# Output projection of the mixer: where its split weights are made, and in which order ACT, DVE and SP issue around it

## The chip, the cores and the metric

The kernel runs on one core of a Trainium2 chip. The metric is the time of one execution on the device in microseconds. The engines are TensorE (PE; its weight loads are a row of their own, PEld), VectorE (DVE), ScalarE (ACT), GpSimd (POOL) and SyncE (SP). SP and POOL issue most of the DMA transfers. Each engine works through its own queue in order, and an instruction that waits holds everything behind it on that engine.

## The reference, cut to what matters

One layer over 512 positions and 1024 channels, all in float32. The part around the change is the projection of the merged branches into the residual, the norm before the MLP, and the MLP's up projection:

```python
merged = gate_a * y_a + gate_b * y_b
x = x + jnp.einsum('bsd,de->bse', merged, w_out[i])

h2 = rmsnorm(x, norm_ffn_g[i])
up = jnp.einsum('bsd,df->bsf', h2, w_up[i])
up = causal_depthwise_conv(up, conv_w[i], conv_b[i])
act = jax.nn.gelu(up[..., :D_FF]) * up[..., D_FF:]
x = x + jnp.einsum('bsf,fd->bsd', act, w_down[i])
```

## The kernel before, in words

**Split operands.** Each float32 product is made of three TensorE products of shorter numbers: an operand is split into a high part (`hi`, a rounded copy made by ACT) and a low part (`lo`, the operand less `hi`), and the product is lo x hi + hi x lo + hi x hi. The low part of a weight is made in one of two ways. Either DVE subtracts (`tensor_tensor` with `ALU.subtract`), or, where the code says `"dma"`, ACT writes `-hi` into the low tile and POOL issues a DMA that adds the raw weight to it (`G.dma_start(lo, raw, accum_op=ALU.add)`). `load_w` (L145) does this for a weight that SP has just loaded; its cast is L153, its negation L156, its accumulating DMA L157, its subtraction L159. `m_split` (L1110) does the same for weights that lie in SBUF: cast L1115, negation L1117, DMA L1118, subtraction L1120. `pieces_T` (L192) loads and splits two pieces of 128 x 1024 for one pair of column blocks of the up projection; its arguments `sub` and `sub2` say how the first and the second piece's low parts are made, and the second goes as the first where `sub2` is left out.

**The projection by seven products.** The 512 x 1024 by 1024 x 1024 projection is a 2 x 2 block product done with seven products in place of eight. `w_out`'s four quarters `b11`, `b12`, `b21`, `b22` lie in two large tiles; `m_combine` forms their sums and differences in place on DVE, and `m_split` splits each. Written order of the weights: w1 and w6 (made during the stage before), w2, w5, w7, w4, w3. `m_product` (L1186) issues one product: two row halves (`rs`), each of four steps (`q`) of three matmuls of 128x512; after a half's last step it calls an evacuation. The activations' operands lie in tiles called slot and quad, the weights in whi/wlo (five pairs) and xhi/xlo (one pair), and the three sets of accumulators are the banks x, y and z. Products that end a row half of the result go through `m_rows` (L1218): DVE adds the bank to the residual x1 (`evac_x1`, L1171), ACT sums the squares (`square_sum`, L457), and `rms_rows` (L460) makes the norm: DVE adds two half sums (L463), a root is made with one ACT instruction between small DVE ones (L386, L391 to L394), and DVE scales the row block by it into `hn` (L468, twice). What `rms_rows` returns, `rest[rb]`, is called later: it transposes `hn` on TensorE (L421), ACT copies the high parts (L380) and DVE makes the low parts (L381) of `h2T`, the up projection's activation.

**What fills the norms' time.** Between those row blocks TensorE gets other work: a product with `w_ple` (`pp`, in steps, evacuated by ACT and stored by POOL), then the first pair's up products. `w_up0` holds the first pair's weights, gate and linear, two pieces each; `early` (L1263) runs them for rows 256 to 511 as soon as row blocks 2 and 3 are normed, and for rows 0 to 255 later.

**The up loop** (its jobs from `up_jobs`, L1320, and `down_jobs`, L1355; the loop at L1445) runs over jobs: for each pair of column blocks a gate job and a linear job, with four jobs of the down projection laid between those of every two pairs. A job's weights are loaded and split one job ahead. Up pieces go through three raw buffers; the down projection's four quarters of 512 KB (L1362) go to one tile and are combined by DVE (L1394, L1395 and so on) and split (`split_w`, L262).

**What sets the order.** The kernel is written in the Tile layer, whose scheduler chooses the order of each engine's instructions when the program is built, except where a `manual_schedule` region names an engine: then that engine issues the region's instructions in the order of the text. Where instructions from outside the region fall among them stays the scheduler's. Before the change one region, from the branch products (L1149) to `manual.close()` (L1274), names PE alone, and the up loop's names PE alone. ACT, DVE, POOL and SP are the scheduler's in both.

Of the kernel before, what the change touches and what calls it, by code (L numbers as in the profile page):

```python
# [15 lines left out]
P = 128  # L16
S = 512
D = 1024
NB = S // P
# [3 lines left out]
DFF = 2816  # L23
# [20 lines left out]
def hybrid_block(  # L44
# [7 lines left out]
    V, A, G, T = nc.vector, nc.scalar, nc.gpsimd, nc.tensor  # L52
# [3 lines left out]
    def kview(w):  # L56
        return w.rearrange("(k p) c -> p k c", p=P)

    w_in_v, w_a_v, w_b_v = kview(w_in[0]), kview(w_a[0]), kview(w_b[0])
    w_out_v, w_up_v, w_down_v = kview(w_out[0]), kview(w_up[0]), kview(w_down[0])  # L60
# [12 lines left out]
    def uid(s):  # L73
        state["n"] += 1
        return f"{s}_{state['n']}"
# [11 lines left out]
    def bank(tag=None):  # L87
        pool, bufs = state["psum"]
        if tag is None:
            tag = state["turn"][state["bank"] % len(state["turn"])]  # L90
            state["bank"] += 1
        return pool.tile([P, 512], F32, tag=tag, name=uid("bank"), bufs=bufs[tag])
# [11 lines left out]
    def tiny(tag, n=1, bufs=4):  # L104
        pool = state["late"] if tag in LATE else small
        return pool.tile([P, n], F32, tag=tag, name=uid(tag), bufs=bufs)
# [38 lines left out]
    def load_w(src, a, b, sub=None, later=None):  # L145


        raw = raw_tile(a, b)
        hi, lo = split_tiles(a, b)
        nc.sync.dma_start(raw, src)  # L150

        def split():
            A.copy(hi, raw)  # L153
            if sub == "dma":

                A.activation(lo, hi.bitcast(F32), AF.Copy, scale=-1.0)  # L156
                G.dma_start(lo, raw, accum_op=ALU.add)  # L157
                return
            (sub or V).tensor_tensor(lo, raw, hi.bitcast(F32), ALU.subtract)  # L159
        if later is not None:  # L160
            later.append(split)
        else:
            split()
        return hi, lo
# [27 lines left out]
    def pieces_T(wv, c0, sub=None, sub2=None):  # L192

        a = load_w(wv[:, 0:4, c0:c0 + 256], 4, 256, sub)
        b = load_w(wv[:, 4:8, c0:c0 + 256], 4, 256, sub2 or sub)
        return [[(*a, 0, 4, c), (*b, 4, 4, c)] for c in (0, P)]
# [186 lines left out]
    def rstd_of(ms, eps_scale):  # L383

        a = tiny("ra")
        V.tensor_scalar(a, ms, -0.5 * eps_scale, -0.5 * EPS, ALU.mult, ALU.add)  # L386
        return newton(a, ms, eps_scale, epst)
# [26 lines left out]
    def transpose_split(src, dst, rb, n=NK, keep=None):  # L414

        done = []
        for k0 in range(0, n, 4):
            w = min(4, n - k0)
            bk = bank()
            for k in range(w):  # L420
                T.transpose(bk[:, k * P:(k + 1) * P], src[:, (k0 + k) * P:(k0 + k + 1) * P], ident)  # L421
            at = (slice(None), slice(k0, k0 + w), slice(rb * P, rb * P + P))
            bk = bk[:, :w * P].rearrange("p (k r) -> p k r", k=w)
            split_out(dst, bk, at)
            done.append((at, bk))
        def copy():
            for at, bk in done:
                A.copy(keep[at], bk)
        return copy
# [24 lines left out]
    def square_sum(bk, src, tag):  # L454

        ss = tiny(tag, bufs=4)
        A.activation(bk, src, AF.Square, accum_out=ss)  # L457
        return ss

    def rms_rows(x_rb, ss, ss1, g_bc, scr, dst, rb, hn=None):  # L460


        V.tensor_tensor(ss, ss, ss1, ALU.add)  # L463
        y = rstd_of(ss, 1.0 / D)
        if hn is None:
            hn = scr.tile([P, D], F32, tag="hn", name=uid("hn"), bufs=2)
        for h in (0, 512):
            V.scalar_tensor_tensor(hn[:, h:h + 512], x_rb[:, h:h + 512], y,  # L468
                                   g_bc[:, h:h + 512], ALU.mult, ALU.mult)
        return lambda: transpose_split(hn, dst, rb)  # L470
# [12 lines left out]
    def quarter(tag, dt=F32R):  # L483

        return ph.tile([P, D], dt, tag=tag, name=uid(tag))
# [13 lines left out]
    ET = mybir.EngineType  # L499
# [112 lines left out]
    with tc.manual_schedule(engines={ET.PE}):  # L612
        proj_N(w_in_v[:, :, 4096:5120], 0, NK, hT, 1, evac_v, rb_outer=False, subs=subs_v1,
               after=forget)
    bk = bk_f[0]
# [29 lines left out]
    sums = [tuple(quarter(f"S{i}{t}").rearrange("p (k r) -> p k r", k=4) for t in "hl")  # L645
            for i in range(1, 5)]
# [67 lines left out]
    with tc.manual_schedule(engines={ET.PE}):  # L714
# [34 lines left out]
        bk = bank("sc")  # L749
# [7 lines left out]
        for g0 in (0, 4):  # L757
            steps(units, 6)
            bk = bank("sc")
# [227 lines left out]
    scr_es, scr = open_pool("scrC", "right")  # L987
# [67 lines left out]
    bk = bank()  # L1055
# [7 lines left out]
    A11, A12, A22, S1, S2, S3, S4 = range(7)  # L1063
# [41 lines left out]
    b11, b12, b21, b22 = b1[:, 0], b1[:, 1], b2[:, 0], b2[:, 1]  # L1105
# [4 lines left out]
    def m_split(b, subs=(None, None), first=None):  # L1110
        res = []
        for j in range(2):
            hi, lo = first if first and j == 0 else split_tiles(2, 512)
            raw = b[:, 2 * j:2 * j + 2]
            A.copy(hi, raw)  # L1115
            if subs[j] == "dma":
                A.activation(lo, hi.bitcast(F32), AF.Copy, scale=-1.0)  # L1117
                G.dma_start(lo, raw, accum_op=ALU.add)  # L1118
            else:
                V.tensor_tensor(lo, raw, hi.bitcast(F32), ALU.subtract)  # L1120
            res.append((hi, lo))
        return res
# [25 lines left out]
    manual = ExitStack()  # L1148
# [6 lines left out]
    scr_es, scr = open_pool("scrD", "right")  # L1155
    x1 = slot(6, F32).rearrange("p (b c) -> p b c", b=NB)
# [9 lines left out]
    gffn = scr.tile([P, D], F32, tag="gbc", name="gffn", bufs=1)  # L1166
# [5 lines left out]

    half = [None] * NB
    rest = [None] * NB

    def evac_x1a(bk, rb, ch):
        evac_x1(bk, rb, ch)
# [8 lines left out]
    def m_product(a, ws, acc, fresh, last, evac=None, qs=range(4), rs=range(2)):  # L1186

        if acc not in m_banks:
            m_banks[acc] = [bank({"x": "mm", "y": "sc", "z": "pt"}[acc]) for _ in range(2)]
        for r in rs:  # L1190
            bk = m_banks[acc][r]
            for q in qs:
                ah, al = (m_at(t, a, q)[:, P * r:P * r + P] for t in range(2))
                wh, wl = (w[:, q % 2, :] for w in ws[q // 2])
                for n, (l, m) in enumerate(((al, wh), (ah, wl), (ah, wh))):
                    T.matmul(bk, l, m, start=(fresh and q == 0 and n == 0),
                             stop=(q == 3 and n == 2), skip_group_check=not fresh)
            if evac:
                evac(bk, r)
# [18 lines left out]
    def m_rows(rows, ch):  # L1218

        def f(bk, r):  # L1220
            rb = rows + r
            evac_x1(bk, rb, ch)
            ss = square_sum(bk, x1[:, rb, 512 * ch:512 * ch + 512], f"s{ch}")
            rest[rb] = rms_rows(x1[:, rb, :], ss, half[rb], gffn, scr, h2T, rb)
        return f

    state["turn"], state["bank"] = ["pt", "pt", "pt", "av"], 0
    w1, w6 = MERGED
# [4 lines left out]
    m_combine(b11, b22, b11, ALU.subtract)  # L1233
    m_product(A12, w2, "x", False, True, qs=range(3))
    m_product(S2, w6, "y", True, False, m_add(2, 0), qs=[3])
    w5 = m_split(b11, (None, "dma"))
    m_product(A12, w2, "x", False, True, m_x, qs=[3])

    A.activation(epst2, half[1], AF.Sqrt)
    w7 = m_split(b12, ("dma", "dma"))  # L1240
    transpose_p(prow, pT, 0)
    m_product(S1, w5, "y", False, False, m_add(2, 1))
    w4 = m_split(b21)
    transpose_p(prow, pT, 2)
    m_product(S3, w7, "z", True, False, m_x2)
    h2T = tuple(k_view(slot(i)) for i in (0, 1))
    w3 = m_split(b22, ("dma", "dma"))
    pp = proj_N_steps(w_ple_v, 0, 2, pT, 1, evac_ple, subs=load_N(w_ple_v, 0, 2, 1))
    m_product(A22, w4, "z", False, True, m_rows(2, 0))
    w_up0 = [pieces_T(w_up_v, 0, V, "dma")]  # L1250
    state["turn"], state["bank"] = ["mm", "mm", "av", "pt", "pt", "pt"], 0
    steps(pp, 16)
    rest[2]()
# [1 line left out]
    state["turn"], state["bank"] = ["pt", "av", "pt", "pt"], 0  # L1255
    m_product(S4, w3, "y", False, True, m_rows(0, 1), rs=[0])
    rest[3]()
    m_product(S4, w3, "y", False, True, m_rows(0, 1), rs=[1])

    w_up0.append(pieces_T(w_up_v, DFF, V, "dma"))  # L1260
    up0 = [[bank(t) for _ in range(2)] for t in ("mm", "sc")]

    def early(n, i, rows=slice(256, S)):  # L1263
        run(proj_T_steps(w_up0[n][i], h2T, up0[n][i], rows))
# [6 lines left out]
    early(1, 1)  # L1271
    for i in range(2):
        early(0, i, slice(0, 256))
    manual.close()  # L1274
    state["turn"] = BANK_TURN
    scr_es.close()
# [5 lines left out]
    scr_es, scr = open_pool("scrE", "right")  # L1282
# [152 lines left out]
    jobs = up_jobs(0, done) + up_jobs(1, done)  # L1435
    jobs[0] = (lambda: w_up0[0], jobs[0][1])
    jobs[1] = (lambda: w_up0[1], jobs[1][1])
    for g in range(N_SEVEN):
        ups = up_jobs(2 * g + 2, done) + up_jobs(2 * g + 3, done)
        for pair in zip(ups, down_jobs(g)):  # L1440
            jobs += pair
    for q in range(2 * N_SEVEN + 2, NF // 2):
        jobs += up_jobs(q, done)

    with tc.manual_schedule(engines={ET.PE}):  # L1445
        ws = jobs[0][0]()
        for n, (_, products) in enumerate(jobs):
            nxt = jobs[n + 1][0]() if n + 1 < len(jobs) else None
            products(ws)
            ws = nxt  # L1450
# [88 lines left out]
    with tc.manual_schedule(engines={ET.PE, ET.Activation, ET.DVE}):  # L1539
        steps(proj_N_steps(w_pg_v, 0, NK, h3T, 1, evac_gate, subs=subs), 72)  # L1540

        rb = NB - 1
        r = ds(rb * P, P)
        for c0 in (0, 256):
            bk = bank()[:, 0:256]
# [53 lines left out]
```

## Time and profile before

| | us |
|---|---|
| median of three timed runs | 946.52 |
| lowest, highest | 944.88, 946.91 |
| the profiled execution | 943.61 |
| its span, first to last instruction | 941.8 |

The profile is of one execution. Its times count from the first instruction of that execution. The span is what the views below divide; what lies around it (1.8 us) is start and end of the execution. In the projection's stage, as the windows of the trace show it, TensorE is busy for 26.04 of the 30 us from 475 to 505 and for 19.95 of the 25 us from 530 to 555. In a timeline's row stand the start, the duration, the engine, the line, the operation, output <- inputs, and how many equal neighbours were merged; in brackets is the engine's idle time before it and what ended that. A line can be that of a helper, and then the tile's name says whose call it is.

### The profile page before, as it was taken

To read this page: it belongs to the slowest core of one execution; us is meant where nothing else is said; L and a number is where in the kernel's file an instruction comes from. 1 tells how busy PE (TensorE), PEld (TensorE's weight loads), DVE (VectorE), ACT (ScalarE), POOL (GpSimd) and SP (SyncE) were. 2 spreads that over 40 slices of the span, in tenths; PEclk is the share of its full clock that TensorE was granted. 3 is DMA by queue.
4 is the path that set the end of the run, shared out by engine and by line. 5 is a ranking of instruction groups with operands and counts; after the bars stand their busy time and mean duration, and the time that the engine had idled before them with its cause. 6 is when DMAs were issued, how large, how long until landed. Compare 5 with 4: busy or idle time off the path is not lost.

```text
span 941.8 us, 12133 instructions
## 1 busy us (share of the span) xinstructions
PE 920.9 (98%) x4375; PEld 767.3 (81%) x4375; DVE 630.2 (67%) x1152; ACT 562.2 (60%) x896; POOL 107.0 (11%) x158
## 2 busy tenths in 40 slices
PE   8999999999999999999998799999999999999996
PEld 7888888888888888888876798888888888888885
DVE  6886999577777767535674447667766767464654
ACT  7745675477677777536566466555555655545633
POOL 1000001400000010001121111010101110100124
PEclk9999999999999999999999989999999999999998
DMA  9533273755444456699777947675866865875422
GB/s 339 187 90 125 66 212 110 237 155 152 120 124 121 115 144 165 218 341 302 165 207 153 300 106 151 179 180 134 200 157 141 216 148 122 218 241 145 108 72 89
DMA packets 110088, 158.98 MB, mean 169 GB/s; under 512 B 6213, under 2 KB 71933, under 8 KB 110029
## 3 DMA queue, kind: packets, MB, share of 16 engines
q1 hardware_dynamic: 96380, 110.73, 36.1%
q0 software_dynamic: 13504, 46.96, 25.2%
q8 instruction: 34, 0.56, 0.2%
q10 hardware_dynamic: 144, 0.52, 0.1%
q14 instruction: 26, 0.20, 0.1%
HBM read 105.74 MB, written 12.62 MB: 126 GB/s over the span
## 4 chain that ended last, share of the span: by engine, by line
PE 90%; DMA 5%; issue 3%; DVE 1%; SPq 0%; ACT 0%; POOL 0%; DVEq 0%; POOLq 0%
PE bank L181 17%; PE bank L183 17%; PE bank L185 17%; PE bank L1375 8%; PE bank L313 3%; PE bank L317 3%; PE bank L320 3%; PE bank L245 3%; PE bank L247 3%; PE bank L243 3%; DMA wlo<-slot 2%; PE bank L905 2%; PE bank L896 2%; PE bank L168 2%; PE bank L169 2%
## 5 line engine op out<-in xcount | busy, mean ns | idle before, releaser
L181 PE MATMUL bank<-slot,wlo 128*128 128x512 f32 (+1 forms) x696 | 273.4, 394 | 0.0
L183 PE MATMUL bank<-slot,whi 128*128 128x512 f32 (+1 forms) x696 | 268.0, 385 | 0.0
L185 PE MATMUL bank<-slot,whi 128*128 128x512 f32 (+1 forms) x696 | 267.7, 385 | 0.0
L185 PEld LDWEIGHTS bank<-slot,whi 128*128 128x128 f32 x696 | 131.7, 189 | 25.2
L181 PEld LDWEIGHTS bank<-slot,wlo 128*128 128x128 f32 x696 | 131.9, 190 | 20.5
L183 PEld LDWEIGHTS bank<-slot,whi 128*128 128x128 f32 x696 | 132.2, 190 | 19.6
L153 ACT CAST whi<-raw 128x1024 fp32r<-128x1024 f32 x95 | 99.4, 1048 | 44.7 <-PE bank L185 15.9
L157 POOL DMA_DIRECT2D wlo<-raw x56 | 48.6, 868 | 539.6 <-ACT wlo L156 354.5
L159 DVE TENSOR_TENSOR wlo<-raw,whi 128x1024 fp32r<-128x1024 f32 x38 | 47.2, 1245 | 28.2 <-ACT whi L153 27.9
L156 ACT ACTIVATE wlo<-whi 128x1024 fp32r<-128x1024 f32 x56 | 59.1, 1059 | 1.0
L1375 PE MATMUL bank<-whi,slot 128*128 128x512 f32 x176 | 56.5, 389 | 0.0
L1288 DVE SCALAR_TENSOR_TENSOR ul<-bank,cvT,ul 128x511 f32<-128x511 f32 x22 | 16.5, 750 | 43.3 <-ACT ul L1287 43.2
L245 PE MATMUL bank<-wlo,slot 128*128 128x512 f32 x106 | 41.7, 394 | 0.1
L243 PE MATMUL bank<-whi,slot 128*128 128x512 f32 x106 | 41.7, 394 | 0.0
L878 ACT ACTIVATE t<-t,mn 128x512 f32<-128x512 f32 (+1 forms) x64 | 35.8, 560 | 9.7 <-DVE mn L875 8.4
L247 PE MATMUL bank<-whi,slot 128*128 128x512 f32 x106 | 41.5, 392 | 0.0
L1287 ACT ACTIVATE ul<-bank,cvT 128x512 f32<-128x512 f32 x22 | 17.1, 779 | 38.3 <-PE bank L185 38.3
L1375 PEld LDWEIGHTS bank<-whi,slot 128*128 128x128 f32 x176 | 33.0, 188 | 6.8
L1382 DVE TENSOR_TENSOR slot<-bank,slot 128x512 f32<-128x512 f32 x48 | 32.5, 683 | 4.7 <-PE bank L1375 4.4
L265 DVE TENSOR_TENSOR wlo<-slot,whi 128x1024 fp32r<-128x1024 f32 x22 | 26.9, 1222 | 12.5 <-ACT whi L264 12.5
L264 ACT CAST whi<-slot 128x1024 fp32r<-128x1024 f32 x22 | 23.0, 1045 | 18.9 <-PE bank L185 15.3
L1375 PE MATMUL bank<-wlo,slot 128*128 128x512 f32 x88 | 34.2, 389 | 0.0
(368 smaller groups left out, 1901.2 us busy)
## 6 DMA issues: line engine op xcount, KB each, us to landing
wlo<-raw POOLq DMA_DIRECT2D x56, 512.0 KB, 5.2
raw<-in_w_up_dram SPq DMA_DIRECT2D x44, 512.0 KB, 4.6
raw<-in_w_in_dram SPq DMA_DIRECT2D x36, 512.0 KB, 3.9
more<-in_w_in_dram SPq DMA_DIRECT2D x20, 512.0 KB, 6.9
slot<-in_w_down_dram SPq DMA_DIRECT2D x16, 512.0 KB, 5.0
raw<-in_w_branch_b_dram SPq DMA_DIRECT2D x8, 512.0 KB, 4.0
slot<-in_w_out_dram SPq DMA_DIRECT2D x4, 1024.0 KB, 9.4
raw<-in_w_branch_a_dram SPq DMA_DIRECT2D x8, 512.0 KB, 7.3
```

Of the source, the lines that this page charges most:

```text
L153: A.copy(hi, raw)
L156: A.activation(lo, hi.bitcast(F32), AF.Copy, scale=-1.0)
L157: G.dma_start(lo, raw, accum_op=ALU.add)
L159: (sub or V).tensor_tensor(lo, raw, hi.bitcast(F32), ALU.subtract)
L181: T.matmul(out_ap, wl, ah, start=(n == 0 and k == 0), stop=False)
L183: T.matmul(out_ap, wh, al, start=False, stop=False)
L185: T.matmul(out_ap, wh, ah, start=False, stop=end)
L243: T.matmul(bk, alo[:, k, r], wh, start=(k == 0), stop=False)
L245: T.matmul(bk, ahi[:, k, r], wl, start=False, stop=False)
L247: T.matmul(bk, ahi[:, k, r], wh, start=False, stop=(k == nk - 1))
L878: A.activation(t, t, AF.Exp, scale=-1.0, bias=m, accum_out=rs[:, i:i + 1])
L1375: T.matmul(bk, l, m, start=(fresh and k == 0 and n == 0), stop=(k == 1 and n == 2), skip_group_check=not fresh)
```

## The change

Five things change.

1. `w5`'s second piece and both pieces of `w7` get their low parts from a subtraction on DVE, not from an accumulating DMA. The same holds for the second pieces of `w_up0`, gate and linear.
2. `m_rows` no longer makes the norm itself. It evacuates and sums squares; the new `m_norm` makes the norm and is called at a written place.
3. From the product with `w4` on, a second region inside the first one names ACT and DVE too, so that the text's order holds for evacuations, norms, splits of `w_up0` and transposes. The linear half of `w_up0` is loaded and split ahead of the second row half of the last product, not after it.
4. `up1`, the gate weights of the second pair, is loaded and split at the end of that region; the up loop takes it from there.
5. The up loop's region names SP beside PE, so that its loads are issued in the text's order.

```diff
@@ m_rows
             rb = rows + r
             evac_x1(bk, rb, ch)
-            ss = square_sum(bk, x1[:, rb, 512 * ch:512 * ch + 512], f"s{ch}")
-            rest[rb] = rms_rows(x1[:, rb, :], ss, half[rb], gffn, scr, h2T, rb)
+            sums[rb] = square_sum(bk, x1[:, rb, 512 * ch:512 * ch + 512], f"s{ch}")
         return f
+
+    def m_norm(rb):
+        rest[rb] = rms_rows(x1[:, rb, :], sums[rb], half[rb], gffn, scr, h2T, rb)
@@ the products
-    w5 = m_split(b11, (None, "dma"))
+    w5 = m_split(b11)
     m_product(A12, w2, "x", False, True, m_x, qs=[3])
...
-    w7 = m_split(b12, ("dma", "dma"))
+    w7 = m_split(b12)
...
-    m_product(A22, w4, "z", False, True, m_rows(2, 0))
-    w_up0 = [pieces_T(w_up_v, 0, V, "dma")]
+
+    manual.enter_context(tc.manual_schedule(engines={ET.Activation, ET.DVE}))
+    m_product(A22, w4, "z", False, True, m_rows(2, 0), rs=[0])
+    m_norm(2)
+    m_product(A22, w4, "z", False, True, m_rows(2, 0), rs=[1])
+    m_norm(3)
+    w_up0 = [pieces_T(w_up_v, 0, V)]
     state["turn"], state["bank"] = ["mm", "mm", "av", "pt", "pt", "pt"], 0
     steps(pp, 16)
     rest[2]()
...
     m_product(S4, w3, "y", False, True, m_rows(0, 1), rs=[0])
     rest[3]()
+    w_up0.append(pieces_T(w_up_v, DFF, V))
     m_product(S4, w3, "y", False, True, m_rows(0, 1), rs=[1])
-
-    w_up0.append(pieces_T(w_up_v, DFF, V, "dma"))
+    m_norm(0)
+    m_norm(1)
+
     up0 = [[bank(t) for _ in range(2)] for t in ("mm", "sc")]
...
     for i in range(2):
         early(0, i, slice(0, 256))
+
+    up1 = pieces_T(w_up_v, 2 * P, "dma")
     manual.close()
@@ the up loop
             jobs += pair
+    jobs[2] = (lambda: up1, jobs[2][1])
     for q in range(2 * N_SEVEN + 2, NF // 2):
         jobs += up_jobs(q, done)
 
-    with tc.manual_schedule(engines={ET.PE}):
+    with tc.manual_schedule(engines={ET.PE, ET.SP}):
```

More of the change, by code (lines that the diff above doesn't have):

```diff
@@ L1174, in hybrid_block @@
     rest = [None] * NB
+    sums = [None] * NB
     def evac_x1a(bk, rb, ch):
```

## The prediction

> **What bounds the kernel now.** I read the page first, then TensorE's idle time by releaser, then the windows of its clock, and last the timelines of the engines around each gap.
>
> ```profile
> span 941.8 us, 12133 instructions
> ...
> PE 920.9 (98%) x4375; PEld 767.3 (81%) x4375; DVE 630.2 (67%) x1152; ACT 562.2 (60%) x896; POOL 107.0 (11%) x158
> ```
>
> TensorE is the bound, so an edit on the other engines is worth only what it changes in TensorE's gaps or clock. In the timeline of TensorE from 460 us on there are three gaps before the tail:
>
> ```profile
> 494.44 0.50 PE L1196 MATMUL bank<-wlo,slot 128*128 128x512 f32 x1 [0.56 <-DMA wlo<-slot]
> ...
> 504.07 0.50 PE L1196 MATMUL bank<-wlo,quad 128*128 128x512 f32 x1 [3.40 <-DMA wlo<-slot]
> ...
> 541.07 1.94 PE L421 MATMUL bank<-ident,hn 128*128 128x128 f32 x8 [5.05 <-DVE hn L468]
> ```
>
> The number in brackets is the idle time. All three lie in the stage that the change edits. The windows (span, busy PE, PEld, DVE, ACT, POOL, then granted clock, DMA share, GB/s) say what they cost beside the idle time, and that nothing of the kind follows:
>
> ```profile
> 505.00:515.00 10.00, 10.00 (x46) 8.29 (x45) 5.92 (x11) 6.67 (x12) 0.00 (x0) 1.00 0.59 149
> ...
> 541.00:542.00 1.00, 0.94 (x5) 0.97 (x6) 1.00 (x2) 0.00 (x0) 0.00 (x0) 0.50 1.01 339
> ...
> 546.00:547.00 1.00, 1.00 (x7) 1.00 (x7) 0.00 (x0) 0.00 (x0) 0.00 (x0) 0.64 0.00 0
> ...
> 600.00:700.00 100.00, 100.00 (x443) 82.84 (x442) 67.83 (x95) 55.25 (x67) 11.17 (x13) 1.00 0.76 183
> 700.00:800.00 100.00, 100.00 (x443) 82.84 (x442) 70.10 (x99) 57.35 (x70) 10.29 (x12) 1.00 0.63 151
> ```
>
> After the gap of 3.40 us the clock stays at 1.00. After the one of 5.05 us it is 0.50 from 541.07 until about 546.72 (a mean of 0.64 in that microsecond is 0.72 us at a half and the rest at one): 5.65 us at half speed, 2.8 us lost. So the stage has 0.56 + 3.40 + 5.05 + 2.8 = 11.8 us to give. From 600 to 800 TensorE is full at clock 1.00: the up loop can give nothing, only take.
>
> The Trainium skill ("TensorE: Matmul & The Clock Gate", section "HAM oscillation — how this bites in real kernels") says not to let TensorE idle for more than about 3.4 us, or its clock is halved. By that rule the second gap stands at the edge and could have cost clock as well; this trace charges it nothing, and by the rule the sum below would be the same, since both gaps go.
>
> **The change, part by part.** *The weights of the sums on DVE (w5's second half, both of w7).* The low part came from an ACT negation and an accumulating DMA that POOL issues:
>
> ```profile
> 485.22 1.89 POOL L1118 DMA_DIRECT2D wlo<-slot  x1
> ...
> 492.97 1.42 POOL L1118 DMA_DIRECT2D wlo<-slot  x1
> ...
> 490.49 1.06 ACT L1115 CAST whi<-slot 128x1024 fp32r<-128x1024 f32 x1 [0.98 <-PE bank L1196]
> ...
> 489.54 1.23 DVE L1120 TENSOR_TENSOR xlo<-slot,xhi 128x1024 fp32r<-128x1024 f32 x1 [3.70 <-ACT xhi L1115]
> 490.68 2.48 DVE L1171 TENSOR_TENSOR slot<-bank,slot 128x512 f32<-128x512 f32 x4
> ```
>
> The first is w5's second half: issued at 485.22, used at 494.44, 9.2 us. The second is w7's: issued at 492.97, used at 504.07, 11.1 us. In place of each stands a subtraction of 1.23 us. w7's second half is cast by 491.55; DVE is in the four evacuations until 493.16, so its low part is there by 494.4 at the latest, where TensorE first asked for it at 500.7 (504.07 less 3.40). w5's cast lies ahead of the issue at 485.22, and DVE has a hole of 3.70 us before 489.54. w7's first half goes the same way and is wanted later than w5's. The three subtractions (3.7 us) fit into holes, and both gaps go: **-3.96 us**. Without the hole, w7's would still have 5 us in hand. Three negations and three DMAs leave too, which I count at nothing.
>
> *The written order through the norms.* This is what ends the third gap now:
>
> ```profile
> 522.76 0.37 SPq L150 DMA_DIRECT2D raw<-in_w_up_dram  x1
> 523.18 2.95 SPq L1362 DMA_DIRECT2D slot<-in_w_down_dram  x3
> ...
> 526.56 0.69 DVE L1171 TENSOR_TENSOR slot<-bank,slot 128x512 f32<-128x512 f32 x1
> ...
> 532.19 1.05 ACT L153 CAST whi<-raw 128x1024 fp32r<-128x1024 f32 x1 [4.84 <-DMA raw<-in_w_up_dram]
> 533.14 0.60 ACT L457 ACTIVATE bank<-slot 128x512 f32<-128x512 f32 x1
> ...
> 538.78 1.23 DVE L1394 TENSOR_TENSOR slot<-slot 128x1024 f32<-128x1024 f32 x1 [3.28 <-DMA slot<-in_w_down_dram]
> ...
> 540.17 1.42 DVE L468 SCALAR_TENSOR_TENSOR hn<-slot,ry,gffn 128x512 f32<-128x512 f32 x2
> ```
>
> Row block 1's last sum is evacuated by 527.25, but its square (L457) stands on ACT behind the cast of an up weight whose transfer lands only at 532.19, and the end of its root (L394, the last step before L468) stands on DVE behind a combination of down weights (L1394) whose transfer lands at 538.78. Both foreign instructions leave: that cast belongs to up1, the second pair's gate weights, now written at the end of the region; and the down weights' loads, which SP issued at 520 to 526, come in the up loop's written SP order behind four up pieces. The chain is then evacuation, square, root, scaling with nothing between. What it costs is seen where it ran without the big holes:
>
> ```profile
> 523.87 0.61 ACT L457 ACTIVATE bank<-slot 128x512 f32<-128x512 f32 x1
> ...
> 524.63 0.16 DVE L463 TENSOR_TENSOR s<-s,s 128x1 f32<-128x1 f32 x1
> ...
> 526.21 0.21 DVE L394 TENSOR_SCALAR ry<-rt,ry 128x1 f32<-128x1 f32 x1
> ...
> 527.17 1.41 DVE L468 SCALAR_TENSOR_TENSOR hn<-slot,ry,gffn 128x512 f32<-128x512 f32 x2
> ```
>
> 0.76 us for the square, 1.8 for the root (524.63 to 526.42), 1.41 for the scaling: with the evacuation 4.7 us, so hn at about 531.3 where TensorE is free at 536.0. Third gap and clock: **-7.85 us**.
>
> *What the written order adds.* Now every ACT and DVE instruction of the region waits its turn, and the up weights' splits stand in it. These start the norms now:
>
> ```profile
> 510.97 0.69 DVE L1171 TENSOR_TENSOR slot<-bank,slot 128x512 f32<-128x512 f32 x1
> ...
> 513.69 0.69 DVE L1171 TENSOR_TENSOR slot<-bank,slot 128x512 f32<-128x512 f32 x1 [0.89 <-PE bank L1196]
> ...
> 522.95 0.69 DVE L1171 TENSOR_TENSOR slot<-bank,slot 128x512 f32<-128x512 f32 x1 [1.27 <-PE bank L1196]
> ```
>
> Less 3.96, row block 2's evacuation starts at 507.0; square, root and scaling end at 511.7. Row block 3's, ready at 509.7, comes only then, and its norm ends at 516.3. Then two subtractions for the first up weights, until 518.7:
>
> ```profile
> L159 DVE TENSOR_TENSOR wlo<-raw,whi 128x1024 fp32r<-128x1024 f32 x38 | 47.2, 1245 | 28.2 <-ACT whi L153 27.9
> ...
> raw<-in_w_up_dram SPq DMA_DIRECT2D x44, 512.0 KB, 4.6
> ...
> wlo<-raw POOLq DMA_DIRECT2D x56, 512.0 KB, 5.2
> ```
>
> (w_up0's four subtractions were two on DVE and two by DMA; all four are DVE's now, so two more of 1.2 us stand in its turn.) Only then come row block 2's low parts (L381), until 520.0. The transposes of row block 3 want one of their banks once S4's first half is through (522.95 less 3.96, and a little before), at 518.8, and get it near 519.4: **+0.6**. Next on DVE and ACT are S4's first evacuation and square (521.4), row block 3's split (523.2), the other two subtractions of w_up0 (525.8), and only then S4's last evacuation, ready at 523.2 (526.56 less 3.96, plus 0.6): done 526.5, square 527.3, root 528.4, scaling 529.1 and 529.8. TensorE has the two early products (2 x 24 matmuls):
>
> ```profile
> 526.36 0.28 PE L181 MATMUL bank<-slot,wlo 128*128 128x256 f32 x1
> ...
> 531.99 0.28 PE L185 MATMUL bank<-slot,xhi 128*128 128x256 f32 x1
> ```
>
> 48 in 5.75 us, so it is done with them near 528.7 and the transposes of row block 0 end 0.8 late: **+0.8**. Row block 1 follows on DVE until 533.0, and TensorE asks for it at 533.1: no gap. The bounds of these two: nothing, if banks and order meet better than that, and 3.4 together, if the turn on ACT and DVE is 1 us later at each place.
>
> *up1, the second pair's gate weights, at the end of the region.* Their casts now wait for row block 1's split, near 535. Cast and negation are 2.1 us a half, the issue 0.9, the landing 5.2 in the median (the row above): 542 and 545. TensorE asks for them after 5 x 2.9 us of 256-wide products from 533.9 on: 548.2 and, for the second half, 550.9. Nothing, with 6 us in hand; at the 9 to 11 us that such landings took above, nothing or 1 us.
>
> *SP's order in the up loop.* A down weight's load now waits behind up pieces, and an up piece behind a down load that waits for its quarter. The loads of the second group and its first product, in the old order, bound it:
>
> ```profile
> 597.72 0.37 SPq L1362 DMA_DIRECT2D slot<-in_w_down_dram  x1
> ...
> 607.73 4.73 SPq L1362 DMA_DIRECT2D slot<-in_w_down_dram  x2
> 618.51 3.28 SPq L150 DMA_DIRECT2D raw<-in_w_up_dram  x2
> 624.28 0.37 SPq L1362 DMA_DIRECT2D slot<-in_w_down_dram  x1
> ...
> 654.15 0.39 PE L1375 MATMUL bank<-xhi,slot 128*128 128x512 f32 x1
> ```
>
> The second up piece of 618.51 (at 621.4) goes behind the down load of 624.28, some 3 to 4 us later, and the down loads of 597.72 and 607.73 go behind the first, to about 619. The product is due at 654.15, with its splits some 10 us before. Nothing, with 20 us in hand; were all of it used up, each microsecond would be TensorE's.
>
> **Sum:** -3.96 - 7.85 + 0.6 + 0.8 = -10.4 us, against the profiled run's own 943.61 us (span 941.8): 933.2. The three timed runs have a median of 946.52, 2.9 above that run; the change comes off alike: **936.1**. At best all 11.8 goes: 934.7.
>
> **The rivals.**
> A, a foreign instruction still stands in the norms. The region orders its own instructions; where the up loop's fall among them is the scheduler's. For it: L1394 stood between two steps of one root. Against: the loads it needs now come late. Then the third gap stays and only the first two go, less the 0.6: 946.5 - 4.0 + 0.6 = 943.1.
> B, up1 comes late: a landing of 11 us, with casts 2 us later than I count. Gate 1 then waits 3 us: 939. Against: the down loads that crowded the DMA at 520 to 540 (share 1.01 at 541) are away.
> C, slower: the last quarter of w_up0 holds the norms. Its load waits for a raw buffer that frees with the first subtraction, near 517.5; its cast is due at 523.4, and S4's last evacuation and both norms now stand behind it. With 4.6 us it lands at 522.1, 1.3 us early. Each microsecond beyond is one of TensorE, plus 2.8 of clock once the gap is as long as the old third one. To give back 10.4 and 1.9 more it must be 10.8 late, a landing of 15.4 us; at 17.5 us the time is 946.5 - 10.4 + 11.6 + 2.8 = 950.5. Against: the longest landing of such a load in this trace is 11.4 us:
>
> ```profile
> DMA to landing us min/median/max: 3.2/4.1/11.4
> ```
>
> D, nothing gained: the first two gaps go, and the written turn opens gaps of 4 us in their place: 946.5.
>
> **How the numbers follow.** Forecast 0.72 (934.7 to 938.5), A 0.11, B 0.08, C 0.04, D 0.05. Run to run the old kernel spreads by 2 us, and about 0.2% (1.9 us) is what a measurement of this kernel can tell from no change. The range runs from 933.0 (all of it, in a low run) to 943.0, which takes in B and part of A and leaves out C, D and the rest. Faster 0.88 (the forecast, B, nearly all of A), same 0.07 (D and a little), slower 0.05.
>
> **What would show it.** Right: no TensorE wait for wlo<-slot in the stage; the clock at 1.00 from 535 to 560; L457 and L394 of the last row block right behind their inputs; the down loads after the fourth up piece; two gaps under 1 us before the transposes. Wrong: a gap over 3.4 us before L421, a clock of 0.50, a wait of L153 in the region for its raw load, or any TensorE gap in the up loop.

## The result, and the profile after

| | before | after |
|---|---|---|
| median of the timed runs, us | 946.19 | 931.67 |
| lowest, highest | 944.88, 946.91 | 931.12, 933.17 |
| the profiled execution | 943.61 | 932.14 |
| its span | 941.8 | 930.0 |

The ratio after to before is 0.9851, with a 95% interval of 0.9834 to 0.9868. The median before is of four runs, one more than ahead of the prediction. The kernel is 14.5 us faster. 10.4 us were forecast, and the median lies under the range's lower end of 933.0. The direction and both mechanisms' places were right, their size was not.

The page of the profile after, its span and TensorE's row:

```profile
span 930.0 us, 12122 instructions
...
PE 919.0 (99%) x4375; PEld 766.9 (82%) x4375; DVE 634.8 (68%) x1157; ACT 556.4 (60%) x891; POOL 102.6 (11%) x153
```

TensorE's busy time falls by 1.9 us only (less half-clock time), the span by 11.8: most of what left is idle time. The windows over the projection's stage after (span, busy PE, PEld, DVE, ACT, POOL, granted clock, DMA share, GB/s):

```profile
490.00:500.00 10.00, 10.00 (x49) 8.29 (x48) 7.78 (x10) 8.33 (x13) 1.60 (x2) 1.00 0.48 82
500.00:510.00 10.00, 10.00 (x45) 8.26 (x44) 5.05 (x11) 5.11 (x11) 1.35 (x2) 1.00 0.74 157
...
530.00:540.00 10.00, 10.00 (x86) 10.00 (x85) 3.86 (x7) 5.85 (x7) 1.75 (x2) 1.00 0.29 54
540.00:550.00 10.00, 10.00 (x74) 9.51 (x73) 5.19 (x8) 7.88 (x9) 1.69 (x2) 1.00 1.02 219
```

No gap is left and the clock is 1.00 throughout. The DMA share from 490 to 500 falls from 1.08 to 0.48. The timelines of DVE, ACT, TensorE and SP at the last row block:

```profile
524.52 0.68 DVE L1171 TENSOR_TENSOR slot<-bank,slot 128x512 f32<-128x512 f32 x1
...
525.24 0.60 ACT L457 ACTIVATE bank<-slot 128x512 f32<-128x512 f32 x1 [2.08 <-DVE slot L1171]
...
529.29 0.21 DVE L394 TENSOR_SCALAR ry<-rt,ry 128x1 f32<-128x1 f32 x1
529.54 1.41 DVE L468 SCALAR_TENSOR_TENSOR hn<-slot,ry,gffn 128x512 f32<-128x512 f32 x2
...
531.83 1.03 PE L421 MATMUL bank<-ident,hn 128*128 128x128 f32 x8
...
505.32 43.66 SPq L150 DMA_DIRECT2D raw<-in_w_up_dram  x8
549.03 3.54 SPq L1374 DMA_DIRECT2D slot<-in_w_down_dram  x4
```

Evacuation and square follow each other, then come row block 0's norm and row block 1's, and nothing foreign stands between. The down weights (L1374, L1362 before) are asked for at 549, not from 520 on. The scaling ends at 530.95, 0.9 us before TensorE transposes its result.

For the experiments one measure is sharper than the whole span: the stretch from the projection's first matmul (L1196, L1197 after) to the second pair's first gate matmul of 128x512. These rows are its ends, first in a second profile of the kernel before (e1 below), then after:

```profile
475.73 1.52 PE L1196 MATMUL bank<-slot 128*128 128x512 f32 x6
...
561.26 0.40 PE L181 MATMUL bank<-slot,wlo 128*128 128x512 f32 x1
```

```profile
475.97 1.29 PE L1197 MATMUL bank<-slot 128*128 128x512 f32 x5
...
547.09 0.40 PE L181 MATMUL bank<-slot,wlo 128*128 128x512 f32 x1
```

The stretch is 85.53 us long before and 71.12 after, 14.41 us less. Behind the stretch, the two kernels take 382.9 us to their end, within 0.1 us. So the whole gain lies in it. In the first profile of before it was 83.59 us.

### The profile page after: what moved, and what is told of

Read it like the earlier page. It is cut to its first block, busy times and chain, and to the rows that moved or that the text cites. A ratio compares the mean times of both kernels' runs of the same rounds, so it can differ in the third digit from the quotient of the medians.

```text
span 930.0 us, 12122 instructions
## 1 busy us (share of the span) xinstructions
PE 919.0 (99%) x4375; PEld 766.9 (82%) x4375; DVE 634.8 (68%) x1157; ACT 556.4 (60%) x891; POOL 102.6 (11%) x153
## 4 chain that ended last, share of the span: by engine, by line
PE 96%; DMA 1%; ACT 1%; DVE 1%; issue 0%; SPq 0%; DVEq 0%; POOLq 0%
PE bank L181 18%; PE bank L183 18%; PE bank L185 18%; PE bank L1387 8%; PE bank L1197 4%; PE bank L313 3%; PE bank L320 3%; PE bank L317 3%; PE bank L245 3%; PE bank L247 3%; PE bank L243 3%; PE bank L905 2%; PE bank L896 2%; PE bank L168 2%; PE bank L169 2%; PE bank L167 2%
## 5 line engine op out<-in xcount | busy, mean ns | idle before, releaser
L1300 DVE SCALAR_TENSOR_TENSOR ug<-bank,cvT,ug 128x511 f32<-128x511 f32 x22 | 16.4, 747 | 26.7 <-ACT ug L1299 26.6
```

## The experiments

All times are medians of timed runs beside the kernel before on the same chip; "stretch" is the one above, from each run's own profile. The profiled executions of e8 and e9 lie 2.9 and 1.8 us above their medians; most of that is ahead of the stretch, which begins at 478.42 and 477.19 there.

| run | edit | us | ratio to before, interval | stretch, us | TensorE's gaps, us |
|---|---|---|---|---|---|
| first profile | before | 946.19 | | 83.59 | 0.56, 3.40, 5.05 |
| e1_before_again | before | 945.89 | 1.0002, 0.9992 to 1.0012 | 85.53 | 0.34, 3.49, 5.39 |
| e2_only_dve | before, sums' weights on DVE | 938.88 | 0.9931, 0.9917 to 0.9946 | 78.79 | 5.84 |
| e10_only_sp | before, SP's written order | 938.48 | 0.9912, 0.9898 to 0.9927 | 77.86 | 0.93, 3.42 |
| e6_dve_sp | before, both of these | 932.46 | 0.9857, 0.9837 to 0.9877 | 71.23 | none |
| e12_two_edits | the same kernel | 932.23 | 0.9844, 0.983 to 0.9857 | 71.26 | none |
| e11_after_again | after | 931.80 | 0.9841, 0.9826 to 0.9855 | 71.09 | none |
| e3_undo_dve | after, sums' weights by DMA | 938.13 | 0.9919, 0.9904 to 0.9934 | 77.16 | 0.40, 3.46 |
| e4_undo_actdve | after, no region for ACT, DVE | 933.40 | 0.9872, 0.9857 to 0.9886 | 72.38 | 0.93 |
| e5_undo_sp | after, no SP order | 940.85 | 0.9946, 0.9922 to 0.997 | 78.52 | 6.00 |
| e7_dve_region | e5, and up1 in the loop | 940.47 | 0.9944, 0.9922 to 0.9965 | 79.48 | 6.71 |
| e8_undo_w7b | after, w7's second half by DMA | 932.56 | 0.9863, 0.9839 to 0.9887 | 72.30 | 0.90 |
| e9_undo_up0 | after, w_up0's second pieces by DMA | 936.36 | 0.9888, 0.9869 to 0.9907 | 76.27 | 3.41 |

### e1: the kernel before, once more

No edit.

> The kernel before, unchanged, for the span and clock of each of its executions. Its first profile had a span of 941.8 us at clock 0.993, 2.6 us under the median of its timed runs. Theory 1 (the clock: in most executions the 3.40 us gap too is followed by half speed): runs near 946 us at a clock near 0.990, runs near 943.5 at 0.993, about 2.8 us for each 0.003 of clock. Theory 2 (the gaps themselves are longer in most executions): spans longer at an unchanged 0.993, with waits of TensorE in the projection that add up to some 12 us, not 9.0. Theory 3 (the difference lies outside the projection): the three gaps and the clock in the projection as in the first profile, and another stage longer.

The profiled execution took 945.99 us, 0.1 over the median of 945.89. TensorE's timeline and windows around its second gap:

```profile
504.30 0.50 PE L1196 MATMUL bank<-wlo,quad 128*128 128x512 f32 x1 [3.49 <-DMA wlo<-slot]
...
543.31 1.94 PE L421 MATMUL bank<-ident,hn 128*128 128x128 f32 x8 [5.39 <-DVE hn L468]
...
504.00:505.00 1.00, 0.70 (x3) 0.58 (x4) 0.00 (x0) 0.00 (x0) 0.00 (x0) 0.91 0.97 176
505.00:506.00 1.00, 1.00 (x4) 0.81 (x3) 0.00 (x0) 0.00 (x0) 0.00 (x0) 0.50 1.10 213
506.00:507.00 1.00, 1.00 (x3) 0.75 (x3) 0.58 (x1) 0.00 (x0) 0.00 (x0) 0.50 1.04 197
507.00:508.00 1.00, 1.00 (x4) 0.77 (x3) 0.12 (x1) 0.72 (x2) 0.00 (x0) 0.50 0.38 70
508.00:509.00 1.00, 1.00 (x6) 0.81 (x5) 0.00 (x0) 0.29 (x1) 0.00 (x0) 0.89 0.04 8
```

A gap of 3.49 us, 0.09 longer than in the first profile, is followed by 3.4 us of half clock (0.18 + 3 + 0.22), 1.7 us lost. The first profile had none. So this execution shows what theory 1 says, with 1.7 us in place of the 2.8 it was given. The stretch is 1.94 us longer than in the first profile: 1.7 by the clock, the rest by gaps that differ by a few tenths. Of the ten runs' clocks five read 0.991, one 0.992 and four 0.993, but the four are not the four fastest (945.22 to 947.75), and none is near the 943.5 that theory 1 forecast for them. What sets the times of those runs no profile here shows.

### e2: the sums' weights on DVE alone

```diff
-    w5 = m_split(b11, (None, "dma"))
+    w5 = m_split(b11)
-    w7 = m_split(b12, ("dma", "dma"))
+    w7 = m_split(b12)
```

> Before, with the sums' weights alone moved to DVE. The two waits of TensorE for wlo<-slot (0.56 and 3.40 us) go in every theory; the third gap stays. Theory 1: the clock loss behind the 3.40 us gap goes too, so -4.0 and up to -2.8 more against the median before: 939.4. Theories 2 and 3: -4.0, or -5 to -6 if the DMA waits are longer in most runs: 940.5 to 942.2. By a rival (the late down weights end the third gap by the DMA's clock, not TensorE's), the 4 us come back as a longer third gap: 944 to 946.

The run is 7.1 us faster than before on the same chip; the stretch is 6.74 us shorter than e1's. The two gaps that are gone added up to 3.8 us in e1, and 1.7 us of clock went with them. About 1.3 us more is a shorter half clock behind the third gap, 3.3 us here to e1's 5.9. The third gap is all that is left, and both things that end it now are seen as before, on ACT, DVE and TensorE:

```profile
528.66 1.05 ACT L153 CAST whi<-raw 128x1024 fp32r<-128x1024 f32 x1 [5.65 <-DMA raw<-in_w_up_dram]
...
535.23 1.23 DVE L1394 TENSOR_TENSOR slot<-slot 128x1024 f32<-128x1024 f32 x1 [3.27 <-DMA slot<-in_w_down_dram]
...
537.51 1.94 PE L421 MATMUL bank<-ident,hn 128*128 128x128 f32 x8 [5.84 <-DVE hn L468]
```

The rival that the gain would come back as a longer third gap falls: that gap grew by 0.45 us.

### e3: after, with the sums' weights by DMA

The diff of e2 undone on the kernel after.

> After, with the sums' weights by the accumulating DMA again. Both waits for wlo<-slot return: 4.0 us over the kernel after in every theory, so 935.7. Theory 1: some executions 2.8 us more with a clock lower by 0.003: up to 938.5. Rival (the norms have slack enough that the delay is hidden later): under 934.

The run is 6.5 us slower than after; gaps of 0.40 and 3.46 us are back, and the clock read 0.93, 0.50, 0.50, 0.50 and 0.86 in the five microseconds from 505 to 510: 3.4 us at half once more. That is theory 1's upper end. The edit is worth about the same with the rest of the change as without it.

### e4, e5, e7: which of the written orders counts

e4 drops the region for ACT and DVE, e5 the order of SP, e7 the order of SP and the early place of up1:

```diff
e4
-    manual.enter_context(tc.manual_schedule(engines={ET.Activation, ET.DVE}))
e5, e7
-    with tc.manual_schedule(engines={ET.PE, ET.SP}):
+    with tc.manual_schedule(engines={ET.PE}):
e7
-    up1 = pieces_T(w_up_v, 2 * P, "dma")
-    jobs[2] = (lambda: up1, jobs[2][1])
```

> After, without the region for ACT and DVE; SP's written order, the places of the norms and of the second pair's weights and the splits on DVE stay. If the late down weights' loads alone made the third gap, it stays away: 932 to 933.5. If ACT's and DVE's order are needed as well (the cast of an up weight ahead of the last square), a gap of 3 to 5 us comes back ahead of the transposes of the last row block, with half clock behind it if it is near 5: 935 to 940.

> After, with SP left to the scheduler in the up loop. If the written order of ACT and DVE with the second pair's weights at its end keeps the norms free: no third gap, 931.5 to 932.5, and the SP order is worth nothing by itself. If the down weights' loads go ahead again and L1394's successor falls into the last root as before (the region orders its own instructions alone): a gap of 4 to 6 us with clock behind it, 937 to 940.

> After, without SP's written order and with the second pair's weights back in the up loop; the region for ACT and DVE, the norms' places and all splits on DVE stay. If foreign instructions can fall into the region (the scheduler's freedom): a third gap of 3 to 6 us, 936 to 940. If the region alone keeps them out: as after, 931.5 to 932.5.

Without the region for ACT and DVE the third gap stays away; a wait of 0.93 us comes at row block 2's transposes, since subtractions for up weights now stand between its root's steps. The stretch is 1.3 us longer than after's. Without SP's order the gap is back at 6.00 and 6.71 us, though ACT and DVE keep their written order. In e5 it has another cause than before, on SP and ACT:

```profile
516.68 1.44 SPq L1374 DMA_DIRECT2D slot<-in_w_down_dram  x3
518.23 0.47 SPq L150 DMA_DIRECT2D raw<-in_w_up_dram  x1
...
529.03 1.04 ACT L153 CAST whi<-raw 128x1024 fp32r<-128x1024 f32 x1 [6.25 <-DMA raw<-in_w_up_dram]
...
531.25 0.68 DVE L1171 TENSOR_TENSOR slot<-bank,slot 128x512 f32<-128x512 f32 x1
...
531.91 1.22 DVE L1406 TENSOR_TENSOR slot<-slot 128x1024 f32<-128x1024 f32 x1
...
534.76 1.51 PE L421 MATMUL bank<-ident,hn 128*128 128x128 f32 x6 [6.00 <-DVE hn L468]
```

Three down weights go ahead of the last quarter of w_up0, whose transfer is issued at 518.23 and lands near 529.0, 10.8 us later. In the kernel after no down weight goes ahead of that transfer; it is issued at 516.53 and cast from 522.1 on. In e5 its cast holds ACT, its subtraction DVE, and S4's last evacuation waits until 531.25. A foreign combination of down weights (L1406) does fall into the root, as rival A had it, but costs little beside that. The late load is the mechanism of rival C. The two together, with the half clock behind the gap, cost 7.4 us of stretch, and they stand open only where SP is not ordered too. e7 shows the same two: a wait of 6.97 us for the load, and L1405 in the root.

### e6, e10, e12, e11: SP's order alone, and the two edits against the whole change

```diff
e10: before, and in the up loop
-    with tc.manual_schedule(engines={ET.PE}):
+    with tc.manual_schedule(engines={ET.PE, ET.SP}):
e6, e12: the same, and the diff of e2
```

> Before, with the sums' weights on DVE and SP's written order in the up loop, nothing else; to be set beside e2_only_dve (938.9, third gap 5.84 us). If the down weights' loads ahead of the up piece are the root of the third gap (they hold L1394 on DVE, and by taking SP and the DMA they make the up piece late that ACT waits for): the gap is gone or under 1 us, 931.5 to 934. If ACT's cast ahead of the last square is enough by itself: a gap of 2 to 4 us stays, 934 to 938.

> Before, with SP's written order in the up loop alone; the sums' weights stay with the DMA. If the third gap (5.4 us) and its half clock (2.9 us) hang on the down weights' loads alone: both go, 8.3 us under the before of the same chip, about 937.7, and e2_only_dve's 7 us add to it to the whole. If the 3.5 us that the norms start later eat the margin that e6_dve_sp showed: a gap of 1 to 3 us stays, 939 to 941.

> Before, with the sums' weights on DVE and SP's written order in the up loop (e6_dve_sp again, timed closer). If the written order of ACT and DVE and the moved up weights are worth nothing: within 0.5 us of e11_after_again. If the cast that still waits for its transfer ahead of the last square takes the margin in some executions: 0.5 to 2 us over it, with a spread wider than after's 2 us.

> The kernel after, unchanged, beside e12 on the same chip. 931 to 932.5, with no gap in the projection.

SP's order alone takes 7.67 us off e1's stretch, the sums' weights alone 6.74; together that is 14.41, as much as the whole change takes off (to the digit by chance, as the half clocks differ by a microsecond between executions). With both edits in one kernel 14.30 and 14.27 are measured. On one chip the two edits' median is 0.43 us over the whole change's (932.23 to 931.80), whose runs spread over 1.4 us: taken together, the remaining edits are worth nothing that these runs can tell. ACT and TensorE in e12:

```profile
527.25 1.05 ACT L153 CAST whi<-raw 128x1024 fp32r<-128x1024 f32 x1 [3.54 <-DMA raw<-in_w_up_dram]
528.21 0.59 ACT L457 ACTIVATE bank<-slot 128x512 f32<-128x512 f32 x1
...
530.85 1.42 DVE L468 SCALAR_TENSOR_TENSOR hn<-slot,ry,gffn 128x512 f32<-128x512 f32 x2
...
532.23 1.04 PE L421 MATMUL bank<-ident,hn 128*128 128x128 f32 x8
```

The up weight's cast still stands ahead of the last square and waits 3.54 us. But its raw load no longer shares the DMA with four down weights. Issued 42.9 us after the stretch's start in e12 as in e2, it lands after 8.1 us here and after 10.2 there. And no combination stands in the root: its last step (L394) follows at once, where in e2 it came 4.4 us after the step before it (L393 ends at 531.96, L394 starts at 536.37). The first half of the scaling is done near 531.6, 0.7 us before TensorE asks for it. So the kernel lives with a margin under 1 us, where the whole change has none of those waits and a margin of 1.6 us at the same place.

### e8, e9: what a single accumulating DMA costs

```diff
e8: after, but
-    w7 = m_split(b12)
+    w7 = m_split(b12, (None, "dma"))
e9: after, but
-    w_up0 = [pieces_T(w_up_v, 0, V)]
+    w_up0 = [pieces_T(w_up_v, 0, V, "dma")]
-    w_up0.append(pieces_T(w_up_v, DFF, V))
+    w_up0.append(pieces_T(w_up_v, DFF, V, "dma"))
```

> After, with the second half of w7 alone by the accumulating DMA. If its 11 us from issue to use were mostly the crowd (two more accumulates and the residual's three ahead of it), it lands in 6 to 8 us now: a wait of 0 to 1 us and no half clock, 931.7 to 933. If the transfer takes its 11 us whatever goes beside it: the wait of 3.4 us comes back, with 1.7 us of clock where the gap is long enough: 935 to 937.

> After, with the second pieces of the first pair's up weights (gate and linear) by the accumulating DMA again. If their two subtractions cost and bring nothing: as after, 931.5 to 932.5. If their place ahead of the row blocks' low parts and the last evacuation matters: 0.5 to 1.5 us under after, 930.5. If the DMA's low parts are late for the early products: a gap of 1 to 4 us, 933 to 937.

POOL and TensorE in e8:

```profile
496.11 1.41 POOL L1118 DMA_DIRECT2D wlo<-slot  x1
...
503.80 0.50 PE L1197 MATMUL bank<-wlo,quad 128*128 128x512 f32 x1 [0.90 <-DMA wlo<-slot]
```

With w5's and w7's other transfers gone, the same low part is used 7.7 us after its issue. In e3, which has those transfers and issues this one at the same place in the stretch, it takes 11.0 us (493.62 to 504.62). A gap of 0.9 us remains and no clock is lost. So some 3.3 us of the 11.0 were the crowd, the other two transfers.

In e9 the third expectation came: the low part of the linear half's second piece is late for an early product. POOL, TensorE, and the clock:

```profile
525.76 0.88 POOL L157 DMA_DIRECT2D wlo<-raw  x1 [4.66 <-ACT wlo L156]
...
535.12 0.50 PE L181 MATMUL bank<-slot,wlo 128*128 128x256 f32 x1 [3.41 <-DMA wlo<-raw]
...
530.00:540.00 10.00, 6.59 (x43) 6.39 (x42) 2.81 (x5) 2.13 (x5) 0.00 (x0) 0.83 0.52 136
```

It takes 9.4 us from issue to use, which makes a gap of 3.41 us, with 3.4 us of half clock behind it. So the two subtractions that I counted only as a burden on DVE save 4.6 us, once the written order has put that split behind row block 3's and the rest has become early enough to need it. In e6 and e12 the same DMA is no hindrance, because the scheduler puts its split earlier: POOL issues it 43.3 us after the stretch's start in e6 and 48.6 in e9.

## Why the prediction was right or wrong

**The first two gaps.** Right in mechanism, too small in size: the term "-3.96" left out the clock. It was read from one execution in which a gap of 3.40 us cost none. Behind the gaps of 3.41, 3.42, 3.46 and 3.49 us in e9, e10, e3 and e1 the clock was halved, and e1's profiled execution is the one that sits at the median. With the 1.7 us of e1 the term is 5.5; undone on the kernel after, it measures 6.1 (e3's stretch less e11's). The prediction set the Trainium skill's rule ("TensorE: Matmul & The Clock Gate", section "HAM oscillation — how this bites in real kernels") beside this gap and said that by it the sum would be the same. That was the error: both gaps go in either case, but by the rule the kernel before had more to lose. Four of the five gaps of about 3.4 us that the traces hold were followed by half clock, as the rule has it; but in e5 the clock was halved 1.88 us into a gap, so they do not show 3.4 us as the least that it takes.

**The idle time in brackets is not the whole cost of a gap.** It counts from the end of the last matmul, 0.39 us after its start for 128x512, while the next in a full row starts after 0.23. Each gap so costs some 0.16 us more than its bracket, and where the clock is full the first matmul behind it 0.1 more. For three gaps that is 0.7 us, an estimate from these starts and durations. With the 11.8 that the prediction found in the stage it makes 12.5, and 12.47 is what the stretch shrank by from the first profile.

**The third gap and its clock, -7.85.** The size held (e10's 7.67 us of stretch). The reason given was two foreign instructions that both had to go. e6 and e12 show that the down loads' place is enough: the cast may stay where it is. Of the 6.5 us by which the scaling comes sooner in e12 than in e2, 4.4 are the combination that left the root and 2.1 the load that lands sooner. That ACT's and DVE's written order has a share in closing this gap was assumed, and is not so: the gap stays away without it (e4). With the rest of the change in place that order is worth 1.3 us, at row block 2.

**The written order's two new waits, +0.6 and +0.8.** They did not come. The step that failed is the root's length: the 1.8 us were read from 524.63 to 526.42, where a low part of the transposes (L381, from 525.10 to 525.79) stood between its steps. In the written order none does, and the chain takes 1.24 us (L463 at 508.54, L394's end at 509.78, in the timeline of DVE after). Only row block 0's takes 1.8 us, for its instruction on ACT stands behind row block 1's square. With two roots 0.55 us too long each, every later step of that sum was put about 1 us too late, and with it both waits.

**up1, and SP's order in the up loop, at nothing.** Right: no gap in the loop, and 382.9 us from the second pair's first gate matmul to the end in both.

**From the profiled run to the median.** I took the 2.9 us between them for a constant that the change leaves alone. In e1 1.7 us of it are the second gap's clock, which the first execution had been spared and which goes with the change. That the timed runs have the same cause is not shown, as they left no trace; but it fits that the kernel after is profiled 0.5 us over its median, not under it.

So the 4.1 us that were missed are 1.4 of waits that did not come, 1.9 of stretch that the first profile lacked (1.7 of it clock), and 0.7 of gap ends; they make 4.0.

**The rivals.** A and C are real mechanisms, seen together in e5 and e7, with C's late load the larger; SP's order shuts both out. B and D did not come.

## What to carry to other kernels

Where one transfer that is needed much later is issued early, look at what it holds up twice: the loads behind it, and the instructions that a scheduler puts on it in a queue that others need. One written queue (SP's) cured here what two others (ACT's and DVE's) did not. And before the clock behind a gap of a few microseconds is priced from one profile, look at a second one: nearly the same gap cost none in one execution and 1.7 us in the next.

## What the runs showed of the hardware that was not expected

Whether a gap costs clock hangs on where it falls, and not on its length alone. In every trace here the clock changes only at times that lie whole multiples of 3.413 us apart; in e1 at 504.82, 508.23, 542.36, 549.19 and 938.31, which are 1, 10, 2 and 114 such steps. Against the kernel's start these steps lie elsewhere in each execution. In the fourteen traces the clock was halved after every step at full clock in which TensorE idled for 1.88 us or more, and after none in which it idled for 1.74 us or less; no step lies between. It came back after a step with 0.71 us of idle time or less, and stayed low after those with 0.95 or more. This is read from the traces; no run was made to test it. The windows of such steps, two of the first profile, then one of e1 and one of e5:

```profile
498.94:502.35 3.41, 1.74 (x9) 1.08 (x7) 1.09 (x2) 2.87 (x4) 1.11 (x2) 1.00 1.07 200
502.35:505.76 3.41, 1.69 (x7) 1.43 (x8) 0.23 (x1) 0.00 (x0) 0.61 (x1) 1.00 1.05 198
...
501.40:504.82 3.42, 0.52 (x2) 0.48 (x3) 0.32 (x1) 0.55 (x1) 0.86 (x1) 1.00 1.03 192
...
527.22:530.64 3.42, 1.54 (x13) 1.34 (x12) 0.53 (x1) 1.04 (x1) 0.00 (x0) 1.00 1.07 372
```

The first profile's gap of 3.40 us was cut by the end of a step into 1.67 and 1.73 us, and cost nothing. e1's gap of 3.49 us had 2.90 us in one step. e5's had only 1.88 us in its first, and the clock fell while TensorE still waited.

The fall can come late: in e1 the gap ended at 504.30 and the clock fell at 504.82, 4.0 us after the gap began, so the loss there lies wholly in work that has already resumed; in e9 and e10 it fell 3.5 and 4.7 us after the gap's begin.

An accumulating DMA of 512 KB took 11.0 us from issue to use in e3, with two more of the weights' ahead of it, and 7.7 us without them in e8.
